# Zero products on TensorE and one ScalarE rounding ahead of the first projections of a hybrid attention block

## The chip, the cores and the metric

The kernel runs on one core of a Trainium2 chip. The metric is device time in microseconds (us) of one execution; a kernel's time is the median of several. Engines are named as in the profile: PE is TensorE's matrix products and PEld its weight loads, DVE is VectorE, ACT is ScalarE, POOL is GpSimd, SP is SyncE, which here only issues DMAs.

## What is computed

One residual block of a decoder over 1024 tokens of width 1024: an RMS norm, one wide input projection, two token mixers side by side (dilated window attention in three groups, and a gated delta rule in chunks), gates, an output projection, and a final norm. Only the very beginning matters here, the norm and the first columns of the projection:

```python
def _rmsnorm(x, w):
    xf = x.astype(jnp.float32)
    y = xf * lax.rsqrt(jnp.mean(xf * xf, axis=-1, keepdims=True) + NORM_EPS)
    return (y * w.astype(jnp.float32)).astype(x.dtype)
...
        h = _rmsnorm(x, norm_w[layer])
        proj = h @ w_in[layer]
        dsa_qkv, dsa_z, gdn_qkv, gdn_z, gdn_b, gdn_a, gate_a, gate_b = _split_columns(proj)
```

## The kernel before

**Precision.** Every large product is made of three fp16 products. A float32 operand is scaled and split into a rounded part ("hi") and the rest ("lo"), and hi·hi, hi·lo and lo·hi are summed in PSUM. For weights, `w_hi` (L165, its instruction at L166) has ScalarE round `st` times 256 into `whi`, and `w_lo` (L168, its instruction in the helper at L83) has VectorE form the rest, `wlo`, from the float32 tile and `whi`. Each works on half of a unit of weights: 128 partitions by 1024 elements. For the activations, `split_rows` (L465) does the same with H_SCALE: ScalarE writes `h_hi` (L469), VectorE `h_lo` (L83), 128 by 512 at a time.

**Order.** TensorE's instructions run in the order in which the program writes them, throughout. In the block from L496 to L564 this holds for VectorE and ScalarE too (`manual_schedule`). All other queues, SP's DMA issues among them, and ScalarE and VectorE after that block, are ordered by a planner at build time, from its own costs and priorities. The stage buffers `wstage` of the loaded weights are two: a third load waits until `w_lo` has read the first.

**The head.** The constants that the norm needs (`cons`, 128 by 136) are loaded on ScalarE's queue, everything else of the head on SP's: the first 128 tokens `xt[0]` in two halves, the two halves of the first weights `stage[0]` and `stage[1]` (the q columns, tiles `wq`), tokens 128 to 383 (`xt[1]`, `xt[2]`), the rest of the constants, the second weights `stage[2]`, `stage[3]` (the k columns, `wk`), `xt[3]`, and the later 512 tokens already transposed (`xs`). Then, from L499:

- VectorE spreads the norm weights over diagonals, `nwd` (L499, TT helper at L86). TensorE multiplies them by ones (L502), two float32 products of 512 columns each, so that every partition of two PSUM banks `nwr` holds the norm weights.
- `rstd_rows(0)` (L444): ScalarE sums the squares of each token's row (L448), adds epsilon (L450) and takes the root (L451); VectorE inverts it (L452).
- `scale_rows(0)` (L454): VectorE multiplies `xt[0]` by that and by `nwr`, a half at a time.
- `turn_rows(0)` (L459): TensorE transposes the 128 tokens in eight float32 pieces into two PSUM banks `pts`, tag "G", of which there are two.
- Weights `stage[0]` are split into `wq`, `pts` into `h_hi` and `h_lo`, and `rows_product` (L472) makes 24 products of 128 columns from a half of the weights: eight of hi·hi, eight with `h_lo`, eight with `wlo`.
- The same for `stage[1]`; then rows 1 and 2 are normalised, transposed, split and multiplied, then the k columns, and so on for 512 tokens by rows and 512 from `xs`.

**The lines of the change.** In the kernel before, the rounding of `stage[0]` stands alone in being done by VectorE:

```python
        pts = turn_rows(0)
        V.tensor_scalar(wq[0][:, 0:4], stage[0], W_SCALE, None, op0=ALU.mult)
        split_rows(0, pts, (0,))
        w_lo(stage[0], *wq, 0)
        split_rows(0, pts, (1,))
        rows_product(q, wq, 0, 0)
        w_hi(stage[1], wq[0], 1)
        w_lo(stage[1], *wq, 1)
        rows_product(q, wq, 0, 1)
```

After the head (from about 41 us on), the kernel is one long stream of products on TensorE: the units of the input projection, fed between the steps of the attention and of the delta rule, then gates, up-projections and the output projection.

Of the kernel before, what the change touches and what calls it, by code (L numbers as in the profile page):

```python
# [11 lines left out]
F16 = mybir.dt.float16  # L12
BF16 = mybir.dt.bfloat16
AF = mybir.ActivationFunctionType
ALU = mybir.AluOpType
# [8 lines left out]
W_SCALE = 256.0  # L24
# [53 lines left out]
def hybrid_block(ctx: ExitStack, tc: tile.TileContext, A):  # L78
    nc = tc.nc
    V, SC, PE, GP = nc.vector, nc.scalar, nc.tensor, nc.gpsimd  # L80

    def STT(out, in0, scalar, in1, op0, op1, eng=None):
        (eng or V).scalar_tensor_tensor(out, in0, scalar, in1, op0=op0, op1=op1)  # L83

    def TT(out, in0, in1, op, eng=None):
        (eng or V).tensor_tensor(out, in0, in1, op)  # L86
# [5 lines left out]
    def bank(tag, bufs):  # L92
        return ps.tile([128, 512], F32, name=f"ps_{tag}", tag=tag, bufs=bufs)


    start = [ctx.enter_context(ExitStack()) for _ in range(2)]
    wst = ctx.enter_context(tc.tile_pool(name="wst", bufs=1))
    sp = start[0].enter_context(tc.tile_pool(name="start", bufs=1))
    spr = start[1].enter_context(tc.tile_pool(name="startr", bufs=1, side="right"))
# [2 lines left out]
    nwd = spr.tile([128, KT, 128], F32, name="nwd")  # L102
    ones0 = spr.tile([128, 128], F32, name="ones0")
    V.memset(ones0, 1.0)

    def load_xt(t, c):
        cs = slice(512 * c, 512 * c + 512)
        nc.sync.dma_start(out=xt[:, t, cs], in_=A["x"][t * 128:t * 128 + 128, cs])
# [46 lines left out]
    def in_turn(i):  # L155

        if last_pe[0]:
            tc.add_manual_dep(i.ins, last_pe[0], order_only, reason="in turn")

    def load_w(src, c, n=256, eng=None):  # L160
        st = wst.tile([128, 4, n], F32, name="wstage", tag="wstage", bufs=2)
        (eng or nc.gpsimd).dma_start(out=st, in_=src[c])
        return st

    def w_hi(st, hi, c):  # L165
        in_turn(SC.activation(hi[:, 4 * c:4 * c + 4], st, AF.Copy, scale=W_SCALE))  # L166

    def w_lo(st, hi, lo, c):  # L168
        STT(lo[:, 4 * c:4 * c + 4], st, W_SCALE, hi[:, 4 * c:4 * c + 4], ALU.mult, ALU.subtract)
# [229 lines left out]
    def add_squares(i, acc, c):  # L399
        eng = V  # L400
        for k in (4 * c, 4 * c + 2):
            dst = acc if k == 0 else sp.tile([128, 2, 256], F32, name="sq", tag="sq", bufs=2)
            SC.activation(dst, xs[i][:, k:k + 2], AF.Square)
            if k:
                TT(acc, acc, dst, ALU.add, eng)
        if c:
            TT(acc[:, 0], acc[:, 0], acc[:, 1], ALU.add, eng)

    def new_acc(i):
        return xt[:, i, 0:512].rearrange("p (a b) -> p a b", a=2)  # L410

    def rstd(i, acc):
        pr = bank("G", 2)
        for tt in range(2):
            PE.matmul(pr[:, tt:tt + 1], lhsT=acc[:, 0, tt * 128:tt * 128 + 128], rhs=ones[:, 0:1],
                      start=(tt == 0), stop=True, skip_group_check=True)
        r = rr[:, 2 * i:2 * i + 2]
        SC.activation(r, pr[:, 0:2], AF.Sqrt, bias=epsc, scale=1.0 / D)
        V.reciprocal(r, r)
        TT(diag, ident[:, None, :].to_broadcast([128, 2, 128]), r[:, :, None].to_broadcast([128, 2, 128]), ALU.mult)  # L420
# [23 lines left out]
    def rstd_rows(t):  # L444

        for c in range(2):
            junk = sp.tile([128, 2, 256], F32, name="sq", tag="sq", bufs=2).rearrange("p a b -> p (a b)")
            SC.activation(junk, xt[:, t, 512 * c:512 * c + 512], AF.Square, accum_out=ss[:, 2 * t + c:2 * t + c + 1])  # L448
        s0, s1 = ss[:, 2 * t:2 * t + 1], ss[:, 2 * t + 1:2 * t + 2]
        SC.activation(s0, s0, AF.Identity, bias=epsc, scale=1.0 / D)  # L450
        SC.activation(s1, s1, AF.Sqrt, bias=s0, scale=1.0 / D)  # L451
        V.reciprocal(s1, s1)  # L452

    def scale_rows(t):  # L454
        for c in range(2):
            x = xt[:, t, 512 * c:512 * c + 512]
            STT(x, x, ss[:, 2 * t + 1:2 * t + 2], nwr[c], ALU.mult, ALU.mult)

    def turn_rows(t):  # L459
        pts = [bank("G", 2), bank("G", 2)]  # L460
        for k in range(KT):
            PE.transpose(pts[k // 4][:, k % 4 * 128:k % 4 * 128 + 128], xt[:, t, 128 * k:128 * k + 128], ident)
        return pts

    def split_rows(t, pts, cs=(0, 1)):  # L465
        for c in cs:
            p = pts[c].rearrange("p (k n) -> p k n", k=4)
            hi, lo = [h[:, 4 * c:4 * c + 4, t * 128:t * 128 + 128] for h in (h_hi, h_lo)]
            SC.activation(hi, p, AF.Copy, scale=H_SCALE)  # L469
            STT(lo, p, H_SCALE, hi, ALU.mult, ALU.subtract)  # L470

    def rows_product(ps_, w, t, c):  # L472

        ts = slice(t * 128, t * 128 + 128)
        for a, b in ((0, h_hi), (0, h_lo), (1, h_hi)):
            for ct in range(2):
                for k in range(4 * c, 4 * c + 4):
                    PE.matmul(ps_[ct][:, ts], lhsT=w[a][:, k, ct * 128:ct * 128 + 128], rhs=b[:, k, ts],
                              start=(a == 0 and b is h_hi and t == 0 and k == 0), stop=(a == 1 and k == KT - 1),
                              skip_group_check=True)  # L480
# [3 lines left out]
    stage = [load_w(src[0], c, eng=nc.sync) for c in range(2)]  # L484
# [11 lines left out]
    with tc.manual_schedule(engines={nc.vector.engine, nc.scalar.engine}):  # L496
        wq, wk = w_first
        q, k = qk
        TT(nwd, ident[:, None, :].to_broadcast([128, KT, 128]), normw[:, :, None].to_broadcast([128, KT, 128]), ALU.mult)  # L499
        nwr = [bank("mm", 3), bank("O", 1)]  # L500
        for c in range(2):
            PE.matmul(nwr[c], lhsT=ones0, rhs=nwd[:, 4 * c:4 * c + 4].rearrange("p a b -> p (a b)"), start=True, stop=True)  # L502
        rstd_rows(0)
        scale_rows(0)
        pts = turn_rows(0)
        V.tensor_scalar(wq[0][:, 0:4], stage[0], W_SCALE, None, op0=ALU.mult)
        split_rows(0, pts, (0,))
        w_lo(stage[0], *wq, 0)
        split_rows(0, pts, (1,))
        rows_product(q, wq, 0, 0)  # L510
        w_hi(stage[1], wq[0], 1)
        w_lo(stage[1], *wq, 1)
        rows_product(q, wq, 0, 1)
        for t in (1, 2):
            rstd_rows(t)
            scale_rows(t)
        pts = turn_rows(1)
        split_rows(1, pts)
        rows_product(q, wq, 1, 0)
        pts = turn_rows(2)  # L520
        rows_product(q, wq, 1, 1)
        w_hi(stage[2], wk[0], 0)
        w_lo(stage[2], *wk, 0)
        split_rows(2, pts)
        w_hi(stage[3], wk[0], 1)
        w_lo(stage[3], *wk, 1)
        rstd_rows(3)
        scale_rows(3)
        for c in range(2):
            rows_product(q, wq, 2, c)  # L530
        for t in range(2):
            rows_product(k, wk, t, 0)
        pts = turn_rows(3)
        acc = [new_acc(0), new_acc(1)]
        for c in range(2):
            add_squares(2, acc[0], c)
        split_rows(3, pts)
        rows_product(k, wk, 0, 1)
        rstd(2, acc[0])
        for c in range(2):  # L540
            add_squares(3, acc[1], c)
        rows_product(k, wk, 1, 1)
        pb = spread(2)
        scale_x(2, pb, 0)
        rows_product(k, wk, 2, 0)
        scale_x(2, pb, 1)
        rows_product(k, wk, 2, 1)
        rstd(3, acc[1])
        for c in range(2):
            split_h(2, c)  # L550
        for c in range(2):
            rows_product(q, wq, 3, c)
        pb = spread(3)
        for c in range(2):
            rows_product(k, wk, 3, c)
        for c in range(2):
            scale_x(3, pb, c)
            split_h(3, c)
        V.tensor_copy(hide_b, hide64)
        V.tensor_copy(ident_b, ident)  # L560
        V.tensor_scalar(cw, convw, 0.5 * P_SCALE, None, op0=ALU.mult)
        q = [bank("mm", 3), bank("O", 1)]
        for ct in range(2):
            quarter(q[ct], wq, ct, 2)  # L564
# [506 lines left out]
    for t in range(8):  # L1071
        tk = slice(t * 128, t * 128 + 128)
        for k in range(KT):
            PE.matmul(pba[:, t * 32:t * 32 + 32], lhsT=h_hi[:, k, tk], rhs=wbas[:, k], start=(t == 0 and k == 0),
                      stop=False, skip_group_check=True)
            PE.matmul(pba[:, t * 32:t * 32 + 16], lhsT=h_lo[:, k, tk], rhs=wbas[:, k, 0:16], start=False,
                      stop=(k == KT - 1), skip_group_check=True)
# [594 lines left out]
    for t in range(8):  # L1672
# [21 lines left out]
        for c2 in range(2):  # L1694
            ch = 2 * t + c2
            ov = ob[:, t, 4 * c2:4 * c2 + 4]
            if ch:

                pwq = [bank("S", 2), bank("S", 2)]
                for i in range(2):  # L1700
                    for q in range(2):
                        for e, hb in ((0, 0), (1, 1), (0, 1), (1, 0)):
# [3 lines left out]
                                      start=(i == 0 and q == 0), stop=True, skip_group_check=True)  # L1706
# [12 lines left out]
            for q in range(2):  # L1719
                for hb, e in ((0, 0), (1, 1), (0, 1), (1, 0)):  # L1720
                    r, c = rows(c2 ^ hb), 2 * hb + q
                    PE.matmul(pS[hb][rows(e), q * 64:q * 64 + 64], lhsT=kdec[r, 2 * c + e], rhs=vn[r, c2, e, q],
                              start=(q == 0), stop=True, skip_group_check=True)
# [6 lines left out]
        for c2 in range(2):  # L1730
            for n, (hb, j) in enumerate(order):
                r, o = rows(c2 ^ hb), (4 * c2 + j) * 64
                PE.matmul(po[r, o:o + 64], lhsT=at[r, hb, j % 2, j // 2], rhs=vn[r, c2, j % 2, j // 2],
                          start=(c2 == 0 and n < 2), stop=True, skip_group_check=True)
# [267 lines left out]
```

## Time and profile before

| | us |
|---|---|
| median of 3 runs | 1076.34 |
| lowest and highest run | 1072.23, 1076.85 |
| the profiled execution's own time | 1075.46 |
| its span, first to last instruction | 1073.7 |
| PE busy in the span | 1048.7 |
| DVE busy, ACT busy | 864.4, 559.6 |

The span is what the views of the trace divide; 1.76 us of the profiled execution lie around it. A row of the timeline gives the start, the time from the start to the end of the last merged instruction, engine, line, operation, output<-inputs, shapes and count. Matrix products are pipelined, so that a row's time is longer than the sum of the distances between starts. In a table of windows the columns are busy time and count for PE, PEld, DVE, ACT and POOL, then the clock granted to TensorE, the busy share of the DMA engines and GB/s.

### The profile page before, as it was taken

What the parts mean: (1) busy time and instruction counts of PE and PEld (TensorE: products, weight loads), DVE (VectorE), ACT (ScalarE), POOL (GpSimd) and SP (SyncE); (2) the same over time, 40 slices, a digit from 0 to 9 for tenths busy, and PEclk for the clock granted to TensorE, in tenths of its full rate; (3) what the DMA queues carried; (4) which work ended last, traced back from release to release, by engine and by line L of the source; (5) the groups of instructions that cost most, each with busy time, mean ns of one, the idle gap of its engine ahead of it and who ended that gap; (6) DMA issues with size and microseconds to landing.
All of it is one profiled execution on the core that took longest, in us unless ns stands there. A gap on an engine that the chain in (4) does not pass through costs nothing.

```text
span 1073.7 us, 23669 instructions
## 1 busy us (share of the span) xinstructions
PE 1048.7 (98%) x9398; PEld 639.1 (60%) x9398; DVE 864.4 (81%) x1982; ACT 559.6 (52%) x1272; POOL 56.1 (5%) x107
## 2 busy tenths in 40 slices
PE   7999999999999999999999999999999999999997
PEld 5995585775956855765645544555545555444443
DVE  6897997869878788979966897986588778899834
ACT  6455766566666656547645623244454345443522
POOL 0000000000000000000000000111200000000000
PEclk9999999999999999999999999999999999999999
DMA  8144531632615432641234357785685433763132
GB/s 278 61 131 106 140 105 50 173 95 80 191 67 149 109 105 61 178 120 50 76 123 159 91 130 196 245 242 158 200 267 166 147 98 121 274 225 109 61 117 79
DMA packets 99488, 148.47 MB, mean 138 GB/s; under 512 B 31136, under 2 KB 64416, under 8 KB 98224
## 3 DMA queue, kind: packets, MB, share of 16 engines
q1 hardware_dynamic: 68976, 84.60, 27.4%
q0 software_dynamic: 12320, 44.11, 13.2%
q10 hardware_dynamic: 18080, 18.23, 4.9%
q8 instruction: 74, 1.21, 0.5%
q14 instruction: 38, 0.31, 0.1%
HBM read 91.13 MB, written 36.90 MB: 119 GB/s over the span
## 4 chain that ended last, share of the span: by engine, by line
PE 61%; DVE 27%; ACT 5%; issue 3%; DMA 2%; SPq 1%; ACTq 0%; DVEq 0%
PE ps_mm L183 15%; PE ps_mm L184 14%; PE ps_mm L185 14%; DVE ca L83 4%; DVE wlo L83 2%; DVE X L86 2%; DVE stmp L86 2%; DVE sm L799 2%; PE ps_S L184 2%; PE ps_S L185 2%; PE ps_S L183 2%; DVE tl L86 1%; PE ps_G L813 1%; DVE rt L86 1%; ACT sm L803 1%
## 5 line engine op out<-in xcount | busy, mean ns | idle before, releaser
L185 PE MATMUL ps_mm<-h_hi,wlo 128*128 128x512 f16 (+1 forms) x552 | 208.3, 377 | 0.0
L183 PE MATMUL ps_mm<-h_hi,whi 128*128 128x512 f16 (+1 forms) x492 | 185.6, 377 | 0.0
L184 PE MATMUL ps_mm<-h_lo,whi 128*128 128x512 f16 (+1 forms) x492 | 185.5, 377 | 0.0
L185 PEld LDWEIGHTS <-wlo 128*128 128x128 f16 x788 | 77.2, 98 | 86.5 <-issue 0.6
L183 PEld LDWEIGHTS <-whi 128*128 128x128 f16 x848 | 83.3, 98 | 69.2 <-issue 0.9
L184 PEld LDWEIGHTS <-whi 128*128 128x128 f16 x848 | 83.2, 98 | 68.0 <-issue 1.2
L183 PE MATMUL ps_mm<-whi,h_hi 128*128 128x256 f16 x384 | 105.1, 274 | 0.0
L185 PE MATMUL ps_mm<-whi,h_lo 128*128 128x256 f16 x384 | 104.7, 273 | 0.0
L184 PE MATMUL ps_mm<-wlo,h_hi 128*128 128x256 f16 x384 | 104.7, 273 | 0.0
L803 ACT ACTIVATE sm<-sm,osb 128x128 f32<-128x128 f32 (+1 forms) x160 | 69.5, 435 | 65.0 <-DVE osb L799 60.5
L86 DVE TENSOR_TENSOR tl<-ps_G,th 128x256 f16<-128x256 f32 (+1 forms) x96 | 52.0, 542 | 21.9 <-ACT th L818 21.4
L83 DVE SCALAR_TENSOR_TENSOR wlo<-wstage,whi 128x1024 f16<-128x1024 f32 x50 | 61.0, 1220 | 3.4 <-ACT whi L166 3.2
L799 DVE CUSTOM_DVE_ANT_0 sm<-ps_S,amask 128x128 f32<-128x128 f32 (+1 forms) x192 | 59.4, 348 | 5.2 <-PE ps_S L792 5.2
L83 DVE SCALAR_TENSOR_TENSOR ca<-xc,cw,ca 128x512 f32<-128x512 f32 x72 | 53.9, 748 | 5.3 <-ACT ca L1010 4.6
L166 ACT ACTIVATE whi<-wstage 128x1024 f16<-128x1024 f32 x49 | 51.4, 1051 | 1.7 <-ACT gst L948 0.8
L83 DVE SCALAR_TENSOR_TENSOR whi<-wstage,whi 128x512 f16<-128x512 f32 x60 | 40.9, 689 | 13.6 <-ACT whi L330 13.0
L813 PE MATMUL ps_G<-cons,sm 128*128 128x128 f32 x280 | 47.9, 275 | 3.1 <-ACT sm L803 1.3
L813 PEld LDWEIGHTS ps_G<-cons,sm 128*128 128x128 f32 x280 | 35.5, 141 | 19.3 <-ACT sm L803 4.9
L184 PEld LDWEIGHTS <-h_hi 128*128 128x128 f16 x384 | 45.8, 119 | 1.6
L330 ACT ACTIVATE whi<-wstage 128x512 f16<-128x512 f32 x60 | 37.1, 627 | 18.4 <-DVE wstage L329 13.3
L183 PE MATMUL ps_mm<-h_hi,wlo 128*128 128x512 f16 x120 | 45.6, 380 | 1.0 <-DVE rx L83 1.0
L183 PEld LDWEIGHTS <-h_hi 128*128 128x128 f16 x384 | 45.6, 119 | 1.5
(445 smaller groups left out, 2593.3 us busy)
## 6 DMA issues: line engine op xcount, KB each, us to landing
wstage<-in_w POOLq DMA_DIRECT2D x68, 512.0 KB, 4.6
og<-osb ACTq DMA_DIRECT2D x32, 132.0 KB, 2.1
og<-og SPq DMA_DIRECT2D x32, 132.0 KB, 2.2
gspb<-gst ACTq DMA_DIRECT2D x16, 256.0 KB, 2.5
sga<-gspa SPq DMA_DIRECT2D x8, 512.0 KB, 6.4
wstage<-in_w_up POOLq DMA_DIRECT2D x8, 512.0 KB, 4.7
wos<-in_w_out SPq DMA_DIRECT2D x8, 512.0 KB, 5.3
sgb<-gspb SPq DMA_DIRECT2D x8, 512.0 KB, 5.1
```

What stands on the lines that cost most here:

```text
L83: (eng or V).scalar_tensor_tensor(out, in0, scalar, in1, op0=op0, op1=op1)
L86: (eng or V).tensor_tensor(out, in0, in1, op)
L166: in_turn(SC.activation(hi[:, 4 * c:4 * c + 4], st, AF.Copy, scale=W_SCALE))
L183: PE.matmul(out, lhsT=wh(k), rhs=mh(k), start=first and i == 0, stop=False, skip_group_check=True)
L184: PE.matmul(out, lhsT=wh(k), rhs=ml(k), start=False, stop=False, skip_group_check=True)
L185: last_pe[0] = PE.matmul(out, lhsT=wl(k), rhs=mh(k), start=False, stop=last and i == len(ks) - 1, skip_group_check=True).ins.name
L330: in_turn(SC.activation(t[:, b, 0], self.part[name], AF.Copy, scale=W_SCALE))
L799: V.tensor_tensor_reduce(P[:, u, :128 * nk], psc[:, u * 256:u * 256 + 128 * nk], mask, -cexp, -NEG, ALU.add, ALU.min, accum_out=osb[:, 256 ...
L803: SC.activation(P[:, u, :128 * nk], P[:, u, :128 * nk], AF.Exp, bias=osb[:, 256 + hd:257 + hd], scale=-1.0, accum_out=osb[:, 260 + hd:261 ...
L813: PE.transpose(pt[:, c:c + 128], P[:, u, i * 128:i * 128 + 128], ident)
```

## The change

Three things, all in the head. A tile of zeros, `idle`, of 128 by 256 32-bit words, read as 512 fp16 columns, is set by VectorE right after the ones. In front of `nwd`, TensorE gets nine fp16 products of it, 128 by 128 weights and 512 moving columns each, into one "G" bank that nobody reads. And the rounding of `stage[0]` goes from VectorE to ScalarE (`w_hi`), ahead of both halves of `split_rows(0)`, and its `w_lo` ahead of them as well.

```diff
     ones0 = spr.tile([128, 128], F32, name="ones0")
     V.memset(ones0, 1.0)
+    idle = spr.tile([128, 256], mybir.dt.uint32, name="idle").bitcast(F16)
+    V.memset(idle.bitcast(mybir.dt.uint32), 0)
...
         q, k = qk
+        warm = bank("G", 2)
+        for i in range(9):
+            PE.matmul(warm, lhsT=idle[:, :128], rhs=idle, start=True, stop=True)
         TT(nwd, ident[:, None, :].to_broadcast([128, KT, 128]), normw[:, :, None].to_broadcast([128, KT, 128]), ALU.mult)
...
         pts = turn_rows(0)
-        V.tensor_scalar(wq[0][:, 0:4], stage[0], W_SCALE, None, op0=ALU.mult)
-        split_rows(0, pts, (0,))
+        w_hi(stage[0], wq[0], 0)
         w_lo(stage[0], *wq, 0)
-        split_rows(0, pts, (1,))
+        split_rows(0, pts)
         rows_product(q, wq, 0, 0)
         w_hi(stage[1], wq[0], 1)
         w_lo(stage[1], *wq, 1)
```

## The prediction

> **What bounds the kernel now.** I read the page first, for how much TensorE idles at all.
>
> ```profile
> span 1073.7 us, 23669 instructions
> PE 1048.7 (98%) x9398; PEld 639.1 (60%) x9398; DVE 864.4 (81%) x1982; ACT 559.6 (52%) x1272; POOL 56.1 (5%) x107
> ```
>
> PE is busy for all but 25.0 us. Windows show where those lie.
>
> ```profile
> 0.00:20.00 20.00, 12.40 (x98) 8.73 (x99) 12.62 (x22) 11.07 (x26) 0.20 (x4) 1.00 0.84 292
> 20.00:100.00 80.00, 79.70 (x806) 67.89 (x805) 71.39 (x109) 42.29 (x60) 4.90 (x9) 1.00 0.43 120
> 1060.00:1073.70 13.70, 5.95 (x39) 3.18 (x37) 5.26 (x13) 3.67 (x11) 0.00 (x0) 0.85 0.20 77
> ```
>
> 7.6 us of the 25.0 are in the first 20 us, 7.75 in the tail, 9.65 scattered between. From 20 us on PE hardly stops, so an earlier start of that stream should move the end by as much. What holds the start is the chain of waits of the first 20 us, in order of time (start, us, what):
>
> ```profile
> 5.39 2.07 PE ps_mm L502 x2
> 7.47 1.71 PE ps_O L502 x2
> 9.17 1.97 PE ps_G L462 x8
> 11.17 0.60 ACT h_hi L469
> 11.77 0.94 ACT whi L166
> ...
> 14.45 1.23 ACT sq L448 x4
> ...
> 16.42 1.15 DVE xt L83 x2
> 17.74 0.69 DVE h_lo L83
> 18.48 1.05 PE ps_mm L478 x16
> ```
>
> The reader is to see three legs: TensorE from 5.39, where `nwd` is ready, to 11.14; ScalarE's queue from 11.17 on, through the squares of tokens 1 and 2; VectorE from 16.42 to 18.43. At 18.48 the first products of tokens 1 wait for the last `h_lo`, and the dense stream begins. VectorE's rounding of the first weights (L506) is not among them.
>
> **TensorE's clock.** The first leg runs slowly. The profile's clock column says 1.00 from the start, but the products speak against it:
>
> ```profile
> 8.11 1.06 PE L502 MATMUL ps_O<-nwd,ones 128*128 128x512 f32 x1
> 8.96 1.06 PE L462 MATMUL ps_G<-cons,xt 128*128 128x128 f32 x4
> 10.92:11.50 0.58, 0.58 (x6) 0.57 (x6) 1.00 1.04 402
> 11.50:12.08 0.58, 0.58 (x13) 0.58 (x11) 1.00 1.06 412
> 19.37 1.04 PE L462 MATMUL ps_G<-cons,xt 128*128 128x128 f32 x8
> ```
>
> The two windows count the products of L478 alone: 6 in 0.58 us, then 13. The rate doubles at 11.5 us. Likewise four transposes take 1.06 us at 8.96, and eight 1.04 us at 19.37. A float32 pass of 512 columns takes 0.85 us from start to start (8.11 to 8.96) in the slow state. Why does it rise at 11.5? The trace has one more slow stretch, in which the clock column shows it:
>
> ```profile
> 735.13:738.55 3.42, 1.99 (x131) 1.56 (x131) 3.12 (x5) 2.44 (x6) 0.00 (x0) 1.00 0.66 259
> 738.55:741.96 3.41, 3.41 (x10) 1.17 (x9) 3.07 (x5) 1.19 (x3) 0.00 (x0) 0.50 0.02 5
> 741.96:745.37 3.41, 3.41 (x77) 2.16 (x76) 0.00 (x0) 1.35 (x4) 0.00 (x0) 1.00 0.38 154
> 4.68:8.09 3.41, 2.70 (x3) 1.17 (x4) 1.41 (x3) 1.07 (x4) 0.00 (x0) 1.00 0.94 336
> 8.09:11.51 3.41, 3.41 (x16) 2.27 (x15) 2.33 (x5) 0.94 (x2) 0.00 (x0) 1.00 1.03 383
> ```
>
> The half-clock stretch is 3.41 us long and ends at once after 3.41 us of full work. From 11.51 to 738.55 are 213 times 3.413 us, so I read a fixed grid of windows, each judged at its end. Windows 4.68 to 8.09 and 8.09 to 11.51 are then the ones judged at the start: 2.70 of 3.41 us (79%) did not raise the clock; the next did, with a hole that its busy time, counting pipelined ends, covers: the eight transposes take from 8.96 to the 10.92 of the next products, 1.96 us, of which 128 columns at a quarter of 0.85 us, eight times, are 1.70. That leaves a hole of 0.26 us, so 92%.
>
> **The change, part by part.** *The zeros.* One memset more on VectorE:
>
> ```profile
> 0.84 0.17 DVE L104 MEMSET ones<- 128x128 f32 x1 [0.84 <-PEq L1994]
> 738.88 0.63 PE L185 MATMUL ps_mm<-h_hi,wlo 128*128 128x512 f16 x1
> 739.30 0.63 PE L183 MATMUL ps_mm<-h_hi,whi 128*128 128x512 f16 x1
> ```
>
> Twice the ones' size, so up to 0.34 us, done at about 1.3, and `nwd` behind it ends at 5.39 only: it costs nothing. The products start at 1.3; the half-clock distance for 512 fp16 columns is 0.427 us (738.88 to 739.30), nine are 3.84 us, end of the stream 5.14. `nwd` comes free at 5.39: 0.25 us of margin, and if that cover is gone (constants earlier, zeros later) `nwd`'s products wait by as much, at most some 0.3 us. The extra "G" bank is written only by PE and in PE's own order, so `turn_rows` waits for nobody new; later "G" tiles swap banks in pairs.
>
> With the zeros every grid window between 1.3 and 9 us is busy but for a hole of 0.25 us ahead of `nwd`'s products, 92 to 93%, as much as raised the clock before and well above what didn't. The first window that suffices may begin up to 0.3 us ahead of the zeros, so the clock rises between 4.4 and 7.8 us by where the grid lies. Without them the same counting from 5.39 gives 8.5 to 11.9, and this profile had nearly the latest case.
>
> *TensorE's leg at full clock.* Four passes of 512 columns at half of 0.85 us, 0.2 for the drain and 0.1 for the first weights: `nwr` done at 5.39 + 2.0 = 7.4, not 9.17. A scaling of half a row follows:
>
> ```profile
> 9.21 0.75 DVE L83 SCALAR_TENSOR_TENSOR xt<-xt,ss,ps_O 128x512 f32<-128x512 f32 x1 [0.96 <-PE ps_O L502]
> 9.88 0.69 DVE L506 TENSOR_SCALAR whi<-wstage 128x1024 f16<-128x1024 f32 x1
> 10.06 0.60 ACT L469 ACTIVATE h_hi<-ps_G 128x512 f16<-128x512 f32 x1 [4.28 <-PE ps_G L462]
> 11.30 1.21 DVE L83 SCALAR_TENSOR_TENSOR wlo<-wstage,whi 128x1024 f16<-128x1024 f32 x1
> 11.66 1.05 ACT L166 ACTIVATE whi<-wstage 128x1024 f16<-128x1024 f32 x1
> 1.64 0.91 SPq L162 DMA_DIRECT2D wstage<-in_w  x2
> wstage<-in_w SPq DMA_DIRECT2D x1, 512.0 KB, 5.9
> ```
>
> It ends at 8.2 (9.96 before), and the last four transposes at 8.85 (11.13 before): 2.28 us earlier.
>
> *The rounding on ScalarE.* It costs 1.05 us instead of VectorE's 0.69, but in the 4.28 us that ScalarE idles ahead of L469. The weights are issued at 1.64 and land 5.9 later, at 7.54: rounding 7.54 to 8.6. Queued behind it are both `h_hi` (0.60 each): 8.6 to 9.8, where they ended at 11.77. So ScalarE, not TensorE, is next: the gain shrinks from 2.28 to 1.97 us. The second half of the weights is rounded from 9.8 to 10.8, not to 12.71. VectorE now waits for ScalarE at `w_lo`, with both `h_lo` (0.69 each) and the second `w_lo` behind it: 8.6 + 1.21 + 1.38 + 1.21 = 12.4. Its next input, the root of tokens 1, comes from ScalarE at 14.45 − 1.95 = 12.5. So VectorE does not take over, by 0.1 us. In the old order at the raised clock it would: 8.2 + 0.69 + 0.69 + 1.21 + 0.69 + 1.21 = 12.7, so of the gain 0.2 us belong to the move. The rounding alone, at the old clock, gains nothing, since ScalarE's queue still starts at 11.17.
>
> *The loads.* The first stage buffer comes free at 9.9 instead of 12.51 (11.30 + 1.21), so the load of the second weights and all behind it on SP's queue can go up to 2.6 us earlier. The tokens that are needed 1.95 us earlier are there:
>
> ```profile
> 2.59 2.35 SPq L108 DMA_DIRECT2D xt<-in_x  x4
> xt<-in_x SPq DMA_DIRECT2D x1, 256.0 KB, 7.3
> 17.39 1.05 ACT L166 ACTIVATE whi<-wstage 128x1024 f16<-128x1024 f32 x1
> 20.01 1.09 ACT L469 ACTIVATE h_hi<-ps_G 128x512 f16<-128x512 f32 x2 [1.57 <-PE ps_G L462]
> ```
>
> The last piece of `xt[2]` has its issue done by 4.94 and lands 7.3 later, by 12.2; its squares would start at 12.5. If the second weights came no sooner than before, their rounding would stay at 17.39 to 18.44 and hold the next `h_hi`, due at 20.01 − 1.95 = 18.06, by 0.4 us; issued 2.6 us sooner, I take nothing for it.
>
> *The sum.* The second `h_hi` is held by ScalarE until 9.2, TensorE's leg ends at 8.85: 0.35 us of it are hidden. Each us that the clock rises after 5.39 costs that leg 0.5, so up to a rise at 6.1 the gain is 1.95 us, and at 7.8 it is 1.1: 1.8 in the mean. Against the profiled execution, 1075.46 − 1.8 = 1073.7. The median of the runs before is 0.88 above that execution, and its runs should have had the rise earlier, at 10.2 in the mean, which would halve the last four transposes (10.01 to 11.13), worth 0.5. I take 1.5, between 1.3 and 1.8, off the median: 1074.8. The three runs of the kernel before lie 4.6 us apart, so this is under what can be told (0.5%, 5.4 us, is about what a measurement of this kernel can tell from no change).
>
> **The rivals.** *The clock rises no earlier.* The lower mark of the judgement is only known to lie between 79 and 92%, and zeros may count for less than data; nothing here shows zeros. Then the gain is 0: 1076.3, at 12%. *Only a window busy throughout counts.* The nine products of 3.84 us hold a whole 3.41 us window in 0.43 of 3.41 positions; in the others the next full one ends no earlier than now, and the time is 1076.3 again. The window to 11.51 had its hole and sufficed, which speaks against it: 8%. [...]
>
> *ScalarE held by the load.* If the first weights land late, ScalarE's strict queue holds both `h_hi` behind the rounding. It decides from a landing after 11.17 − 0.60 − 1.05 = 9.5; at 12.2, as late as `xt[2]`, it costs 2.7 us: 1079.0. The row says 7.54: 5%.
>
> *A new order by the planner.* From 41 us on VectorE and ScalarE run in an order worked out from costs at build time, and the changed head may shuffle the evictions that PE waits for. The scattered idle is 9.65 us: doubled, less the gain, 1076.3 + 9.65 − 1.5 = 1084.5; it outweighs the gain from 1.5 us of new waits on, and exceeds 0.5% from 7. Removed, 1065.2. Little speaks for it, since the program's own order is unchanged: 13%, evenly.
>
> **How the numbers follow.** The forecast has 62%. Its gain of 1.1 to 1.95 from the median, less half the spread of the runs (2.3) and some room for the planner, gives 1070.5; no gain and the upper half of the spread, less what the forecast's weight takes back, 1078.2. Faster by over 0.5% needs 1071.0: half of the planner's 13%, and a low draw, 8%. Slower, above 1081.7: 5%. Within: 87%.
>
> **What would show it.** L502's two products taking some 2 us, `h_hi` ending near 9.8, L478's first row of tokens 1 (18.48) starting near 16.6, PE dense from there, the same waits of PE after 41 us. Wrong: L502 still at 3.8 us; a rise at the old place; `h_hi` waiting for DMA; new PE waits by VectorE after 41 us.

## The result, and the profile after

The kernel after took 1078.99 us in the median of 14 runs (1074.92 to 1081.96), the kernel before 1076.28 (1072.23 to 1078.46, 14 runs beside them): a ratio of 1.0028, 95% interval [1.0016, 1.0041]. That is within the 0.5% that the forecast called no change, but on the other side of it: 2.7 us more where 1.5 us less were forecast. The profiled execution of after took 1078.73 us.

From the page after, the span and the busy times:

```profile
span 1076.9 us, 23689 instructions
PE 1050.5 (98%) x9407; PEld 639.1 (59%) x9407; DVE 864.2 (80%) x1982; ACT 560.5 (52%) x1273; POOL 56.4 (5%) x107
```

TensorE has nine products and nine weight loads more, which are 18 instructions, and nothing else of size has changed. The head of after, in the timeline of PE and then of ACT (start, time, what, wait):

```profile
1.33 3.75 PE L503 MATMUL ps_G<-idle 128*128 128x512 f16 x9 [1.33 <-DVE epsc L142]
5.20 1.12 PE L507 MATMUL ps_mm<-nwd,ones 128*128 128x512 f32 x2
6.16 1.02 PE L507 MATMUL ps_O<-nwd,ones 128*128 128x512 f32 x2
...
16.53 0.38 PE L480 MATMUL ps_mm<-h_lo,whi 128*128 128x128 f16 x4 [0.98 <-DVE h_lo L83]
```

```profile
7.80 1.06 ACT L168 ACTIVATE whi<-wstage 128x1024 f16<-128x1024 f32 x1 [1.78 <-DMA wstage<-in_w]
8.76 1.06 ACT L471 ACTIVATE h_hi<-ps_G 128x512 f16<-128x512 f32 x2
```

The zeros end at 5.08, `nwd`'s products (L507, before L502) end at 7.18 and no longer at 9.17, `h_hi` ends at 9.82, and the dense stream starts at 16.53 instead of 18.48: 1.95 us earlier, as forecast. So the loss lies behind the head. The waits of PE from 728 to 746 us, in before and in after (total, times, longest):

```profile
PE ps_G L1365 <- DVE Y L86: 1.4, 2, 1.0
```

```profile
PE ps_G L1369 <- DMA MT<-u_d: 2.4, 1, 2.4
PE ps_S L1354 <- issue: 2.0, 1, 2.0
```

This is the second of two merges in the delta rule (`merge`, L1343, before L1339). In its middle, 128 small products of 32x32, 256 instructions with their weight loads, run in a burst of about 1.05 us. TensorE now waits for `MT` and then stands still for 2.0 us inside the burst, waiting for nothing that the profile shows; such an idle stretch, which the profile puts down to "issue", is called a stall from here on. The clock's windows there, in before and in after (the first product count is PE's; the number behind POOL is the granted clock):

```profile
736.00:739.00 3.00, 2.14 (x129) 1.60 (x130) 2.69 (x5) 2.52 (x6) 0.00 (x0) 0.92 0.46 182
739.00:742.00 3.00, 3.00 (x9) 1.03 (x8) 2.66 (x4) 0.79 (x2) 0.00 (x0) 0.51 0.02 5
742.00:746.00 4.00, 4.00 (x81) 2.50 (x80) 0.00 (x0) 1.92 (x5) 0.00 (x0) 1.00 0.32 131
```

```profile
736.00:739.00 3.00, 1.31 (x119) 1.24 (x119) 1.90 (x3) 0.56 (x1) 0.00 (x0) 0.92 0.05 14
739.00:742.00 3.00, 0.96 (x6) 0.46 (x6) 0.64 (x1) 0.57 (x1) 0.00 (x0) 0.50 0.00 0
742.00:746.00 4.00, 4.00 (x12) 1.50 (x11) 1.50 (x3) 1.30 (x3) 0.00 (x0) 0.58 0.23 92
```

The reader is to see PE's 0.96 us of work in the second window and the clock: it stays at half until 745.36 instead of 741.96, so that full work runs slowly for another 3.4 us. What released the products is in the DMA view of 737.6 to 741.2 us (a strip of 40 slices of 0.09 us, and the queues):

```profile
DMA  0000000000060000000000000000000000000000
GB/s 0 0 0 0 0 0 0 0 0 0 0 182 0 0 0 0 0 0 0 0 0 0 0 0 0 0 0 0 0 0 0 0 0 0 0 0 0 0 0 0
q8 instruction: 1, 0.02, 1.7%
```

The only transfer in all this time is one packet of queue 8, which the view calls "instruction", at 738.6. TensorE seems to have waited for its next instructions; the experiments test that.

A ledger says where else the gain went. Both programs issue the same instructions on TensorE in the same order, so each one's start can be subtracted from its counterpart's (traced starts, the added ones left out; us, minus is earlier than in before's profile):

| start in before | what stands there | after | 256 instr. (13) | 274 instr. (14) |
|---|---|---|---|---|
| 22.98 | dense stream | −1.94 | −1.57 | −2.20 |
| 530.05 | ahead of a wait for `og` | −2.39 | −2.24 | −0.97 |
| 543.46 | behind it | −0.96 | −2.00 | +0.76 |
| 672.41 | first merge, in the burst | −0.96 | −2.01 | +0.75 |
| 676.59 | behind the burst | −0.35 | −2.02 | +1.30 |
| 736.43 | second merge, start of the burst | −1.38 | −2.49 | +0.87 |
| 737.94 | in the burst | +0.57 | −2.49 | +0.87 |
| 743.77 | behind it, clock up again | +3.33 | −3.54 | +5.46 |
| 982.07 | output projection | +3.27 | −3.57 | +5.38 |

In after the gain is carried for 500 us and even grows by 0.45. Then 1.4 of it is lost at 530 us and 0.6 in the first merge; 1.0 comes back before the second merge, where 2 are lost at the wait for `MT` and 2.8 in the stall with its half-clock stretch. The loss at 530 us has this row on VectorE, which before's profile has not:

```profile
DVE md L877 <- DMA og<-og: 1.1, 1, 1.1
```

### The profile page after: what moved, and what is told of

Its sections match the earlier page's. It is cut to its first block, busy times and chain, and to the rows that moved or that the text cites. A ratio compares the mean times of both kernels' runs of the same rounds, so it can differ in the third digit from the quotient of the medians.

```text
span 1076.9 us, 23689 instructions
## 1 busy us (share of the span) xinstructions
PE 1050.5 (98%) x9407; PEld 639.1 (59%) x9407; DVE 864.2 (80%) x1982; ACT 560.5 (52%) x1273; POOL 56.4 (5%) x107
## 3 DMA queue, kind: packets, MB, share of 16 engines
q8 instruction: 74, 1.21, 0.5%
## 4 chain that ended last, share of the span: by engine, by line
PE 60%; DVE 26%; ACT 4%; DMA 4%; issue 3%; SPq 1%; DVEq 0%; ACTq 0%
PE ps_mm L185 15%; PE ps_mm L187 14%; PE ps_mm L186 14%; DVE ca L83 3%; DVE wlo L83 2%; DVE X L86 2%; DVE sm L803 2%; DVE stmp L86 2%; PE ps_S L186 2%; PE ps_S L187 2%; PE ps_S L185 2%; DVE tl L86 2%; DVE rt L86 2%; PE ps_G L817 1%; ACT sm L807 1%
```

## The experiments

Theory A, a supposition from that packet which the runs are to test: TensorE's instructions are fetched in blocks of a fixed number. The 18 more shift the block ends against the program, one of them into the last products of the merge's burst, where the next block isn't there in time. Rivals: B, the earlier stream (or whatever else comes with the zeros) meets other transfers badly; C, the moved rounding costs; later D and E, the number of instructions as such. Ratios are to the kernel before, run beside it on the same chip, with 95% intervals; diffs are to the kernel after unless said otherwise.

**1. The zeros alone.** The rounding stays on VectorE in the old order:

```diff
-        w_hi(stage[0], wq[0], 0)
+        V.tensor_scalar(wq[0][:, 0:4], stage[0], W_SCALE, None, op0=ALU.mult)
+        split_rows(0, pts, (0,))
         w_lo(stage[0], *wq, 0)
-        split_rows(0, pts)
+        split_rows(0, pts, (1,))
```

> The nine zero products with the rounding left on VectorE. Theory A (18 more instructions on TensorE's queue shift where its instruction blocks end; one block then ends inside the burst of small products of the merge near 738 us and costs 2.0 us there, 'issue' in the waits; what the head gains is lost at the waits for DMA ahead of it): L502's two products in 2 us, first products of tokens 1 some 1.7 to 1.9 us earlier than 18.48, the 2 us issue wait in the merge as in the changed kernel, time 1 to 3 us above before. Theory B (starting the stream earlier makes later loads meet other transfers; no instruction block is involved): the same head, no long issue wait, time anywhere from 2 below to 3 above before by which load is late. Theory C (the rounding on ScalarE costs it): 1.5 to 2 us below before.

1077.32 us, 1.0006 [0.999, 1.0022]. The head came out 2.3 us early, and the profiled execution, at 1072.14 the lowest of its runs, had no stall at all in the second merge, against A's expectation, and one of 0.6 us in the first. The median is 5 us above that execution. With 18 instructions the stall of the second merge comes in some executions and not in others, as run 4 shows too; what the untraced executions had is not known.

**2. The rounding alone.** The kernel before with the moved lines, no zeros.

> The rounding and its order moved, no zero products: no instruction more on TensorE and no faster clock. Theories A and B: first products of tokens 1 at 18.5 as before, no issue wait in the merge, time as before within 0.15%. Theory C (the rounding on ScalarE costs): 2 to 3 us above before, as the changed kernel.

1077.12 us, 1.0006 [0.9992, 1.002]: nothing gained or lost, and the head unchanged (0.16 us). C falls, as far as the move alone goes. Its profile has a short stall behind the burst, in the projection's products, which the counts below explain:

```profile
PE ps_mm L183 <- issue: 0.8, 1, 0.8
```

**3. The instructions alone.** The kernel before with the zero tile and nine products of 16 columns, which take little time (thirty of them start within 0.8 us, 1.3 to 2.1, in run 6; the diff is to the kernel before):

```diff
+    idle = spr.tile([128, 256], mybir.dt.uint32, name="idle").bitcast(F16)
+    V.memset(idle.bitcast(mybir.dt.uint32), 0)
...
+        warm = bank("G", 2)
+        for i in range(9):
+            PE.matmul(warm[:, :16], lhsT=idle[:, :128], rhs=idle[:, :16], start=True, stop=True)
```

> Before with nine zero products of only 16 columns ahead of the first work, so 18 instructions more on TensorE, the 'G' banks swapped and the zero tile set, but the clock not raised and the rounding on VectorE. Theory A: head as before (18.5), an issue wait of about 2 us in the merge near 738 us, time 2 to 3 us above before. Theory B: no such wait, time as before within 0.15%.

1079.58 us, 1.0035 [1.0022, 1.0049]: the whole loss, with a head only 0.6 us earlier and the rounding where it was. Its waits of PE from 728 to 746 us:

```profile
PE ps_G L1370 <- DMA MT<-u_d: 2.6, 1, 2.6
PE ps_S L1355 <- issue: 2.4, 1, 2.4
PE ps_G L1370 <- DVE Y L86: 0.3, 1, 0.3
```

**4. The kernel after, again.**

> The changed kernel once more, for a second trace of it. Theory A: the issue wait of 2 us returns at the same instruction of the merge; the wait for the load of MT ahead of it may differ in length. Theory B: both waits differ from the first trace, by chance; time 0.1 to 0.4% above before either way.

1079.09 us, 1.003 [1.0017, 1.0043]. Its profile, again of the fastest of its runs (1077.34), has a wait of 3.0 us ahead of the burst, where after waits for `MT`, and no stall behind it: A's expectation for this trace failed.

**5. Two instructions.** As 3, with `range(1)`.

> The kernel before with the zero tile and one product of 16 columns in the head: 2 more rows of TensorE instead of 18, the same bank taken, the same order of loads, the rounding on VectorE. Theory A (18 rows move the end of an instruction block into the last rows of the merge's burst of 32x32 products): the block end lies 16 rows behind the burst, no issue stall in it, ratio 1.000 (0.999 to 1.001). Theory B (whatever else comes with the zeros costs: the bank, the order of the loads, other meetings of transfers): as with 18 rows, ratio 1.0035.

The ratio is 1.0 [0.9981, 1.0018]. The tile, the bank and the order of loads are those of 3, and the loss is gone: B, as far as it put the cost there, falls.

**6. Sixty instructions.** As 3, with `range(30)`.

> The kernel before with thirty products of 16 columns: 60 more rows of TensorE, rounding on VectorE. Theory A: the block end that falls into the burst is again the same one (about 190 rows into it instead of 232), but the block ahead of it now begins some 40 rows ahead of the burst, in the projection's products of the 3 us before the wait for MT, so the block is asked for before the wait and is there in time: no issue stall over 0.5 us in the burst, ratio 1.000 (0.998 to 1.001). A variant of A, in which any block end in the burst costs its 2 us: ratio 1.003. Theory D (each further row costs time): 1.0035 x 60/18, that is 1.01.

The ratio is 0.9996 [0.9977, 1.0016], and no stall in the merges of its profile is over 0.2 us. Sixty instructions cost less than 18: D falls.

**7. The change with 72 instructions.** The same clock time of zeros, cut finer:

```diff
-        for i in range(9):
-            PE.matmul(warm, lhsT=idle[:, :128], rhs=idle, start=True, stop=True)
+        for i in range(36):
+            PE.matmul(warm[:, :128], lhsT=idle[:, :128], rhs=idle[:, :128], start=True, stop=True)
```

> The kernel after with its zeros cut into 36 products of 128 columns: 72 rows instead of 18 for the same 4,608 half-clock cycles and so the same clock. Theory A: head as in after (first products about 1.9 us earlier), no issue stall in the merge's burst, so 1.5 to 2.5 us below the kernel after; against the kernel before 0 to 1.5 us less, by what the waits for transfers at 534 and 736 us take back: ratio 0.9985 to 1.000. Theory B (the earlier stream itself meets the transfers badly): as after, 1.003.

1074.31 us, 0.9978 [0.9961, 0.9994]: faster than before, and better than A expected. The stream is early as in after (1.55 us), the loads are issued in after's order, and here it pays. The profile has no stall in the second merge and one of 0.6 us in the first.

**8. The change with ten instructions.**

```diff
-        for i in range(9):
-            PE.matmul(warm, lhsT=idle[:, :128], rhs=idle, start=True, stop=True)
+        zero = idle.bitcast(F32)
+        for i in range(2):
+            PE.matmul(warm, lhsT=zero[:, :128], rhs=zero[:, None, :].to_broadcast([128, 2, 256]), start=True, stop=True)
+        PE.matmul(warm, lhsT=idle[:, :128], rhs=idle, start=True, stop=True)
```

> The kernel after with the same clock time of zeros from two float32 products of 512 columns and one float16 product (10 rows or fewer instead of 18). Theory A: the block end lies 8 rows behind the last row of the burst's place in after, that is at its very end or just behind it; no stall or one hidden by the projection's products behind the burst, ratio 0.9985 to 1.0005. Theory B: as after, 1.003.

The ratio is 1.0012 [0.9992, 1.0032], which is neither expectation. Its profile has no stall in the merges, but 2.3 us of waiting for `MT` and a half-clock window. The run is inconclusive.

**9 and 10. The same filler ahead of or behind the burst.** 27 products of 16 columns in the second merge, in 9 ahead of its first left products, in 10 ahead of its last right ones (there with `g == 1` and `pu`):

```diff
             Y = p2_.tile([128, 16, 32], F32, name="Y", tag="rv", bufs=3)
+            if hb == 1 and g == 0:
+                for n in range(27):
+                    PE.matmul(py[:, :16], lhsT=h_hi[:, 0, 0:128], rhs=h_hi[:, 0, 0:16], start=True, stop=True,
+                              skip_group_check=True)
```

> The kernel after, head untouched, with 27 products of 16 columns (54 rows of TensorE, 0.2 to 0.5 us) put just ahead of the first left products of the second merge; their results are overwritten. Theory A (place of the block end in the burst): the block end still falls into the burst, but the block before it is now entered some 55 rows ahead of the burst, ahead of the wait for MT, as with the 72 rows of zeros; no issue stall, 0.9975 to 0.9995 of the kernel before, some 3 us below the next kernel. Theory B (the zeros cut into shorter products made the 72 rows good): as the kernel after, 1.003.

> The same 27 products put behind the burst, ahead of the last right products of the second merge: the same number of instructions, the same work, the same blocks behind them. Theory A: the burst stands to its block end as in the kernel after, so the issue stall of 2.0 to 2.4 us is there in most executions, 1.002 to 1.004. Theory B: 1.003 too, so only the pair tells them apart.

Ahead 0.9996 [0.9986, 1.0006], behind 1.0021 [1.0008, 1.0034]: the same work and head, and the ratios are 0.0025 apart. The profile of 9 has no stall in the burst, that of 10 one of 2.1 us. The 3 us expected between them were 1.4 in the medians; the profile of 9 has a wait of 3.1 us for `MT`, which that of 10 has not, so part of the saving may have gone there.

**11. More work ahead of the burst.** As 7, and in the second merge

```diff
-        feed.tick(MERGE_TICKS)
+        feed.tick(MERGE_TICKS + 4 * hb)
         for _ in zip_longest(left(1), right(0)):
...
-        feed.tick(UW_LAG[1][hb])
+        feed.tick(UW_LAG[1][hb] * (1 - hb))
```

> The 72 rows of zeros of the faster variant, and in the second merge 9 steps of the projection instead of 5 ahead of the burst (the 4 behind the merge are left out for it, so that all that follows meets the same steps): TensorE then works for 2.6 us more while MT still lands. Theory A with the wait for MT as the second cost: the wait of 1.0 to 3.0 us shrinks under 0.5 us, no half-clock window in the merge, 1 to 2.5 us below the next best, ratio 0.9955 to 0.998. Rival (the wait moves): state_parts behind the merge then meets its own loads without steps ahead of it, and the gain is taken back: 0.9975 to 0.999.

The ratio is 0.9974 [0.9965, 0.9983], which can't be told from that of 7. The profile shows no wait ahead of the burst, where 7's had 1.8 us for `Y`, but 1.2 us of waiting for `MT`'s copy behind the merge (L1417). By the profile the rival, that the wait moves, is the nearer one. A stall of 1.3 us stands in the first merge.

**12. The zeros alone with 72 instructions.** 7 with 1's order.

> The 72 rows of zeros with the rounding left on VectorE in the old order. If the move of the rounding brings anything at the end, this is slower than the 72 rows with it (0.9978); with the head 0.25 us earlier than with the move, as the run with the clock alone showed (8.91 against 9.16 for the first whi product), 0.997 to 0.999, not to be told from 0.9978: the rounding is worth nothing beside the clock. That the clock alone and 18 rows gave 1.0006 was then the luck of its wait.

1073.05 us, 0.997 [0.9958, 0.9982], the lowest ratio of all: without the rounding's move the change pays as well. (The first `whi` product starts at 8.79 us in run 1 and at 9.39 in after.) From 1, with the same order on every queue and 18 instructions, it is 0.0036 apart.

**13, 14 and 15. A whole block, and a block and 18.** `range(128)` of 36 columns (256 instructions), `range(137)` of 34 (274), and 256 with 1's order, in the form of 7's diff.

> The kernel after with its zeros cut into 128 products of 36 columns (256 instructions of TensorE, about 4.3 to 4.9 us of them). Theory A (place within blocks of 256 instructions): every later instruction has the place in its block that it had in the kernel before, so no stall is added in the bursts of either merge; the head's gain of 1.3 to 2.0 us is kept but for what the transfers at 534 us take: 0.9970 to 0.9990. Theory E (it is the number of instructions: the more, the better or the worse): the same as with 274.

> The same with 137 products of 34 columns: 274 instructions, 18 more than a whole block. Theory A: block ends fall into the bursts as in the kernel after, an issue stall of 2.0 to 2.4 us in most executions and longer half-clock stretches: 1.0015 to 1.0035. Theory E: within 0.0005 of the run with 256.

> The 256 instructions of zeros with the rounding left on VectorE in the old order. If the rounding has no share, within 0.001 of the run with 256 instructions and the rounding moved; by the difference of the two clock-only pairs so far (1.0006 to 1.0029 and 0.9970 to 0.9978) it may be 0.0005 to 0.002 faster. Theory A for the head and the bursts as there: 0.9965 to 0.9985.

The ratios are 0.9982 [0.997, 0.9994] with 256, 1.0024 [1.0011, 1.0037] with 274, and 0.9993 [0.9977, 1.0008] with 256 in the old order, the last a little worse than expected. Nine short products more, which end no later (5.24 us against 5.31), cost 0.0042, or 4.5 us: it is the place within blocks of 256 instructions. E falls. One thing else differs between 13 and 14, the order in which the planner issued the loads of the second weights and the last tokens on SP's queue; within each of the sets 3, 5 and 6; after, 4, 7, 9 and 10; 1 and 12, every queue has one order, and they show the same cost.

On the rounding the runs disagree: 15 is above 13 (with another order of loads), 12 below 7, and 1 is 0.0022 and 0.0024 below after and 4, with intervals that overlap. Whether its move has a share beside 18 instructions is not settled.

Counts show the blocks directly. In all of after, 74 packets of 16,384 bytes ran on queue 8, and TensorE's trace has 18,943 instructions, semaphore and drain instructions included: 255.99 for each packet. The next two views have windows from 0 to the start and to the end of a stall, in after (preceded by the end of its stall of 0.4 us in the first merge) and in the run with 274 (the first number in brackets counts products of PE, each with its weight load):

```profile
0.00:672.27 672.27, 658.55 (x5687) 443.44 (x5687) 559.47 (x1351) 395.86 (x956) 31.92 (x64) 1.00 0.42 121
0.00:739.10 739.10, 722.85 (x6579) 477.56 (x6579) 617.94 (x1468) 420.05 (x998) 40.32 (x78) 1.00 0.46 132
0.00:741.06 741.06, 722.85 (x6579) 477.56 (x6579) 617.94 (x1468) 420.05 (x998) 40.32 (x78) 1.00 0.45 132
```

```profile
0.00:739.30 739.30, 723.67 (x6707) 479.87 (x6707) 616.67 (x1467) 420.06 (x998) 40.16 (x78) 1.00 0.46 132
0.00:742.59 742.59, 723.67 (x6707) 479.87 (x6707) 617.72 (x1468) 420.06 (x998) 40.16 (x78) 1.00 0.46 131
```

After's stall stands behind its 6579th product, as do the stalls of 3 and 10; in 14, with 256 instructions more than after, it stands behind the 6707th, 128 products on. From the first merge's stall to the second's are 892 products, 1784 instructions, and with the 8 semaphore instructions that the trace has between them 1792, seven times 256. The short stall of run 2, which has no instruction added, also stands behind the 6579th product; there this is 12 instructions behind the burst. By this count the block ends 10 instructions behind the burst in 5, 2 behind it in 8 and 48 ahead of its end in 6.

## Why the prediction was wrong, point by point

*Right.* The zeros' time, the clock (the two passes at 6.16 take 1.02 us, where before's at 7.26 took 1.92), `nwr` done at 7.18 for 7.4, `h_hi` at 9.82 for 9.8, the stream 1.95 us earlier; the rounding worth nothing alone; the planner's order of VectorE, ScalarE and GpSimd untouched behind the head. On SP's queue it put the second weights ahead of the last tokens (10.14 us for 12.54, so 2.4 us earlier where up to 2.6 were counted). That zeros count as work for the clock, which the first rival doubted, holds (0.43 us from pass to pass behind them, 0.85 without); so does a gain, of about 2 us, in the variants whose block ends lie elsewhere (0.9978 with 72 instructions, 0.9982 with 256). Two small slips are in the sums: 8.6 + 1.21 frees the first stage buffer at 9.8, not 9.9, and the mean of the gains between 1.1 and 1.95 comes out at 1.7, not 1.8. Neither matters to the result.

*Not borne out.* That 0.2 us of the gain belong to the move: the stream came 2.32, 1.85 and 1.05 us earlier in the old order (runs 1, 12 and 15) and 1.54 to 2.20 with the move (after, 4, 7, 13 and 14), so these profiles show no such share.

*Wrong, the step that failed.* "From 20 us on PE hardly stops, so an earlier start of that stream should move the end by as much." I took the small idle share for proof that nothing behind the head has a time or a place of its own. Two things have. One is a place: each instruction's position in a block of 256. The forecast gave the zeros a price in time (nothing, rightly) and none for being 18 instructions ahead of all others. Runs 3, 5, 6 and the pairs 9 and 10, 13 and 14 show this cost: about 0.0035 for the 18 alone, 0.0042 to 0.005 between the change with 18 or 274 and with 72 or 256. In before, the block ends 12 instructions behind the burst, among large products; 18 more put that end 6 instructions ahead of the burst's end. A burst of 1.05 us doesn't cover the 3.5 us that passed in after from the landing of `MT` to the next block's products. The 256 is from the counts above. In run 4 the block's packet ran at 735.45, 4.65 us ahead of its first instructions at 740.10, and there was no stall; in the profiles of after, 3 and 14 the stall was 2.0, 2.4 and 3.4 us.

The other is time: a wait for transfers, which takes an early stream back. At 530 us it took 1.4 us in after; at `MT` the stream came 1.38 us earlier and left 0.57 later. The times from issue to landing of the four loads of `MT`, in before and in after:

```profile
DMA to landing us min/median/max: 6.2/8.8/9.1
```

```profile
DMA to landing us min/median/max: 4.9/8.1/12.3
```

The last one lands 12.3 us after its issue, but as late a landing occurs with no instruction added (12.3 in run 2), so it is not shown to be the change's doing. The forecast's sign that "the same waits of PE after 41 us" would show it right was the right place to look.

*The rivals.* None of mine was this one. The one nearest, "a new order by the planner", sought the loss in new waits after 41 us, but by another cause, and the orders that it named, those of VectorE and ScalarE, are the same. The range to 1078.2 left 1078.99 out for want of a rival in which added instructions cost by where they push the others.

*Open.* In the profiles of 1 and 4 the packet with the block ran at the start of the wait for `MT` or ahead of it (733.49 for a wait from 733.43, 735.45 for one from 736.14), in those of after and 3 some 1.1 us after `MT` had landed. That wait stands 18 instructions behind the start of the block before, so it may be a near thing; what decides it was not found. Nor was it tried what makes `MT` and `og` late, nor whether the loss at 530 us has to do with blocks too: the profiles of the runs with 2, 10 and 256 instructions lose up to 0.25 us there, those with 18, 60, 72 and 274 lose 0.5 to 1.8, except that of run 1, which loses nothing.

## What to carry to other kernels

Instructions added at the head of this long unrolled stream moved the later block ends on TensorE: 18 and 274 cost about the same (1.0028 and 1.0024), and 256 did not (0.9982). So count added instructions modulo 256, the block in these traces (the remainder tells how far the ends move), and look at where the bursts of many short instructions lie; a filler of a whole block (run 13), or a finer cut of the same work (run 7), tells in one run whether this is the cost. An earlier start is worth what the waits for transfers leave of it (at 530 us they took 1.4 of 2.4 us in after): follow the same instruction through both traces instead of comparing shares of idle time.

## What the runs showed of the hardware

The wait of PE put down to "issue" in mid-burst, with one packet on the instruction queue in it, was a block that wasn't there. In after, `MT` was there at 737.55, the packet ran at 738.6, products resumed at 741.07, 3.5 us from the end of the wait against 1.05 us for the burst. From the start of the packet to the products were 2.44 us in after, 2.70 in 3, 2.44 in 10 and 2.24 in 14, though the packet itself took about 1 us. In run 14 it ran only at 740.36, 1.2 us into the stall, which came to 3.4 us. In after the idle time was paid twice, since the clock then stayed at half for one more window: the windows from 738.53 on, with 1.37 and 3.42 us of work at 0.50:

```profile
738.53:741.94 3.41, 1.37 (x47) 0.82 (x35) 0.58 (x1) 0.52 (x1) 0.00 (x0) 0.50 0.02 5
741.94:745.36 3.42, 3.42 (x9) 1.21 (x8) 1.56 (x3) 1.35 (x4) 0.00 (x0) 0.50 0.08 31
745.36:748.77 3.41, 3.41 (x77) 2.17 (x76) 0.00 (x0) 0.88 (x2) 0.00 (x0) 1.00 0.31 127
```

The windows that the forecast read are in the records of the granted clock. In before these begin at 11.51 us and change at 738.55, 741.96 and 1069.64, which is 213, 1 and 96 times 3.413 us; in after they begin at 4.67 and change at 738.53, 745.36 and 1073.04, 215, 2 and 96 times 3.413. Where the windows lie differs from profile to profile, as the forecast's means suppose: the half-clock stretch of the second merge begins at 738.55 in before and, by the clock's shares in the windows of 3 us there, at about 736.2 in 8, 740.1 in 3 and 740.7 in 4.

Products of zeros raised the clock as others did: behind the nine of 3.75 us, float32 passes of 512 columns follow each other after 0.43 us from 5.73 on in after, and after 0.85 us from 6.41 on in before. And one execution was without a stall that another of the same kernel has: of the two profiled executions of after only the slower one (1078.73, against 1077.34) has it.
